# A hybrid decoder layer: the delta rule's outputs turned by VectorE instead of TensorE, one read back from memory, and a plan with other durations

## The chip, the cores and the metric

The kernel runs on one core of a Trainium2 chip. Its time is device microseconds from the start of the program to its end; the lower the better. Five engines work side by side, each on its own queue of instructions in order: TensorE (PE in the profile; it multiplies matrices, PEld is its weight load), VectorE (DVE), ScalarE (ACT), GpSimd (POOL) and SyncE (SP, which here only starts transfers). Transfers between the chip's memory (DRAM) and the on-chip memory (SBUF) run on 16 DMA engines. TensorE writes to PSUM, which VectorE and ScalarE read.

## What is computed

One decoder layer on 512 tokens of width 1024, in float32: a half-weighted SwiGLU block (width 2816), a mixer, a second SwiGLU block and a final norm. The mixer is one wide projection whose columns feed two branches:

- HGRN2: 8 heads of a gated linear recurrence, in chunks.
- Gated DeltaNet, the delta rule: 8 query/key heads and 16 value heads of 128, a causal short convolution on q, k and v, a decay for each head, and a chunked solve of a unit lower triangular system.

The part that the change touches is the second branch. In the reference, cut to what matters:

```python
T = triangular_solve(eye + A, eye, lower=True, unit_diagonal=True)
u = T @ (v * beta[..., None])
w = T @ (kb * exp(gam)[..., None])
def step(S, inp):                       # over the chunks of a head
    v_new = u_c - w_c @ S
    o = (q_c * exp(gam_c)[..., None]) @ S + qk_c @ v_new
    S = S * exp(g_end) + k_to_end.T @ v_new
...
o_g = rmsnorm(o_g, gdn_out_norm) * silu(gz)
y_g = o_g @ w_branch_gdn
y = sigmoid(gate_h) * y_h + sigmoid(gate_g) * y_g
```

## The kernel before, in words

Every float32 operand of a large product is split into a high and a low part of a rounded float32 type, and each product is three passes, high by high, low by high and high by low (`mm3`, L188 to L191). ScalarE makes the high part of a weight slab of 128 x 512 (`act.copy`, L1773) and VectorE the low part by a subtraction (L1783). For "folded" slabs ScalarE writes the negated high part instead (L1776), and a transfer started by POOL adds the slab from DRAM to it (L1779), so that VectorE has nothing to do. `folded` (L1789) decides: before, every second slab of the weights for k, q, v and z (48 slabs).

The layer has three stages: the first SwiGLU block (`ffn`), the mixer, the second block. The mixer is written as some 100 threads (Python generators) that ask for engines with a duration, for buffers and for events. `Desk` (L64 to L138) runs them against the durations that they state and so writes out, when the kernel is built, the order of the instructions on each engine; at run time the engines go through that order and wait for each other by semaphores. The durations are therefore what decides what stands where. `V` and `A` (L761, L762) give VectorE's and ScalarE's time from the number of elements, `T_` states TensorE's, and `LAG` (L52) the time that is left for transfers: `turn` for each leg of a detour through DRAM, `fold` for the adding transfer of a folded slab, `back`, `out`, `m` and others.

TensorE's dense products come from `product` (L1792) and `closing` (L1611), in a line that `loader` and `choose` set (weights through three raw buffers). Around them run the eight units of the delta rule (two value heads each):

- `g_n` (L1179) multiplies keys and queries (L1214) and masks the results on VectorE (L1218, L1220) and scales them (L1229).
- `g_b` (L1239) stores the four diagonal 32 x 32 blocks to DRAM, reads them back with a system in each partition (`gfs<-nb`, L1253) and the identity (L1259), and POOL solves them in 31 pairs of operations (L1265, L1266), whose time is stated as .78 + .0045 n w. The matrix has one buffer, `m`: unit u+1 is loaded when unit u has been solved (event `P`).
- `g_inv` (L1276) turns the solution on VectorE (L1284, L1291) and doubles it on TensorE twice, to blocks of 64 and 128 (L1308, L1318, L1331, L1339).
- `g_rec` (L1352) runs the recurrence over four chunks: L1393 and L1394 (state by keys and queries), L1397, L1406, L1411, L1420 and L1422, and the new state in L1433. Then the outputs are scaled by ScalarE (L1457), turned to the other layout by four TensorE transposes for each head (L1464), gated by VectorE (L1468) and stored (`keep`, `od<-on`); `operand` (L1545) reads them later for the branch's second product.
- The values come out of the convolution (`conv`, L1091) with channels in the partitions and are needed with tokens in them. VectorE turns blocks of 32 x 32 (`turn`, L1126), and `bounce` (L1128) stores the result (L1132) and reads it back in four transfers of a quarter each (L1138); `g_w` (L1269) multiplies it by its rate (L1273).

Of the kernel before, what the change touches and what calls it, by code (L numbers as in the profile page):

```python
# [8 lines left out]
F32 = mybir.dt.float32  # L9
F32R = mybir.dt.float32r  # L10
I32 = mybir.dt.int32
AF = mybir.ActivationFunctionType
ALU = mybir.AluOpType
# [4 lines left out]
T = 512  # L18
NT = T // P
D = 1024  # L20
# [28 lines left out]
STAY = (15,)  # L49
CONVS = 7  # L50
SLACK = 0.8
LAG = dict(raw=3.5, gb=6.5, nb=6, m=7, out=5, back=6, turn=2.5, fold=4.5)  # L52
EASE = 2.5
LANES = {"a": 2, "b": 2, "d": 1, "e": 1}

# [632 lines left out]
def mixer(tc, mp, e):  # L688
# [31 lines left out]
    for size, names in ((1024, "n2:2 gz:2 fs:1 ut:1"), (512, "kn:3 gm:1 qm:2 gb:2 ln:1 at:4 vb:4 t64:2 on:2"),  # L720
                        (256, "ft:1 tp:1 thg:2 x:1 we:1 s:3 w:1"), (128, "fm:1"), (64, "sm:4")):
        for it in names.split():
            n, b = it.split(":")
# [34 lines left out]

    D = Desk(wx0=1, wx1=1, wx2=1, wx3=1, mm=2, a=2, b=2, d=1, e=1, ta=TA, tm=6, thg=1, raw=RB, w=WB, n2=2, gz=2, fs=1, ut=1, t=3, kn=3, gm=1,
             qm=2, gb=2, ln=1, mi=3, mt=3, at=4, vb=4, t64=2, on=2, ft=1, x=1, we=1, w_=1, s=3)  # L760
    V = lambda n: ("use", "DVE", 0.21 + 0.001 * n)  # L761
    A = lambda n: ("use", "ACT", 0.2 + 0.0009 * n)  # L762
    T_ = lambda n: ("use", "PE", n)
    S = ("use", "SP", 0.4)

# [357 lines left out]

    def turn(out, x):

        dve.transpose(out.rearrange("p (f c j) -> p c f j", f=4, c=NT), x)  # L1126

    def bounce(name, x, out, tag=None):  # L1128

        yield S  # L1130
        scr = dr.tile([P, T], F32, name=name)
        sp.dma_start(scr, x)  # L1132
        yield "lag", LAG["turn"]
        if tag:
            D.put(tag)
        for f in range(4):
            yield S
            sp.dma_start(out[32 * f:32 * f + 32].rearrange("p (r a) -> p r a", r=4),  # L1138
                         scr.rearrange("(r i) (f a) -> f i r a", i=32, f=4)[f])
        yield "lag", LAG["turn"]  # L1140

    def g_e(u, st):
# [96 lines left out]
    def g_b(u, st):  # L1239


        n2 = st["n2"]
        nb = dr.tile([4, 8, 32, 32], F32, name=f"nb{u}")
        for b in range(4):
            r = slice(32 * b, 32 * b + 32)
            yield S
            sp.dma_start(nb[b].rearrange("s i j -> i s j"), n2[r, :, :, r].rearrange("p a c j -> p (a c) j"))
        yield "lag", LAG["nb"]
        yield "on", *([("P", u - 1)] if u else ["m"])
        m = G["m"][0]  # L1250
        for b in range(4):
            yield S
            sp.dma_start(m[32 * b:32 * b + 32].rearrange("p i j -> p (i j)"),  # L1253
                         nb[b].rearrange("s i j -> s (i j)").unsqueeze(0).to_broadcast([4, 8, 1024]))
        yield "on", ("t12", 0) if u % 3 else ("t0", 0)
        yield "get", "t", 1
        t = st["t"] = G["t12"][0][:, u % 3 - 1] if u % 3 else G["t0"][0]
        yield S
        sp.dma_start(t, eye4)  # L1259
        yield "lag", LAG["m"]  # L1260
        for j in range(31):
            n, w = 31 - j, j // 4 + 1
            yield "use", "POOL", .78 + .0045 * n * w
            tv = v3(places["fm"]("fm", (P, 96))[:, :n * w], n)
            pool.tensor_tensor(tv, bc(m[:, j + 1:, j], w), t[:, j:j + 1, :w].to_broadcast([P, n, w]), op=ALU.mult)  # L1265
            pool.tensor_tensor(t[:, j + 1:, :w], t[:, j + 1:, :w], tv, op=ALU.add)  # L1266
        D.fire(("P", u))
# [84 lines left out]
    def g_rec(u, st):  # L1352
# [99 lines left out]
        for i in range(2):  # L1452
            yield "get", "on", 1
            ons.append(places["on"]("on", (P, NT, P)))
            for c in range(NT):
                yield A(150)
                act.activation(ons[i][:, c], at[i][:, c], AF.Copy, scale=rho[:, 4 * i + c:4 * i + c + 1])  # L1457
        D.fire(("R", u))
        for i in range(2):
            yield "get", "b", 1  # L1460
            yield T_(Patient(.5))
            pt = ps("pto", "b")
            for c in range(NT):
                pe.transpose(pt[:, c * P:(c + 1) * P], ons[i][:, c], ident)  # L1464
            yield "on", ("z", 2 * u + i)
            yield V(560)
            og = ons[i].rearrange("p c b -> p (c b)")
            dve.scalar_tensor_tensor(og, pt, cs[:, C_GN:C_GN + 1], gz[:, i * T:i * T + T], op0=ALU.mult, op1=ALU.mult)  # L1468
            D.put("b")
            if i:  # L1470
                D.fire(("Z", u))
            if u == 7:
                yield "on", "projected"
                yield A(512)
                k = 14 + i
                a, b = so[k] = uh[:, k - 8], ul[:, k - 8]
                act.copy(a, og)
                yield V(512)
                dve.tensor_tensor(b, og, a.bitcast(F32), op=ALU.subtract)
                D.fire(("so", k))  # L1480
                continue
            D.start((6, u), keep(od[2 * u + i], og, "on", ("od", 2 * u + i)))

    def keep(to, tile_, tag, event=None):

# [22 lines left out]
    def zgate(i, pt):  # L1508

        yield "get", "ta", 1  # L1510
        yield *V(512), 1
        o = ta("zg")
        dve.tensor_tensor(o, pt, rbc, op=ALU.mult)
        D.put("mm")
        g = G["gz"][i // 2 % 3].rearrange("p c b -> p (c b)")[:, i % 2 * T:i % 2 * T + T]
        yield A(512)
        act.activation(g, o, AF.Tanh, scale=0.5)
        yield V(512)
        dve.scalar_tensor_tensor(g, g, 1.0, o, op0=ALU.add, op1=ALU.mult)
        D.put("ta")  # L1520
        D.fire(("z", i))
# [23 lines left out]
    def operand(k, wait, get, make):  # L1545

        yield "on", *wait
        if get:
            yield "get", get, 2
        yield "on", ("od", k), *([("so", k - 2)] if k > 10 else [])  # L1550
        yield "get", "ta", 1
        yield S
        og = ta("og")
        sp.dma_start(og, od[k])
        yield "lag", LAG["back"]
        if k > 8:
            yield "on", "projected"
        yield *A(512), 1
        a, b = so[k] = make()
        act.copy(a, og)  # L1560
        yield *V(512), 1
        dve.tensor_tensor(b, og, a.bitcast(F32), op=ALU.subtract)
        D.put("ta")
        D.fire(("so", k))

# [45 lines left out]
    def closing():  # L1611

        for d, q in wbgs:
            if q == 0:
                yield "get", "mm", 1
            yield "on", ("slab", (("m", d), q))
            hi, lo = made[("m", d), q]
            for j in range(4):
                k = 4 * q + j
                yield "on", ("so", k)  # L1620
                yield T_(.69)
                if k == 0:
                    pts[d] = psd.tile([P, T], F32, tag="mm", name="pmm")
                c = slice(j * P, (j + 1) * P)
                mm3(pts[d], hi[:, c], lo[:, c], *so[k], k == 0, k == VH - 1)
            D.put("w")
            if q == 3:
                D.fire(("wbg", d))
# [158 lines left out]
        D.fire(("slab", key))  # L1787

    def folded(k, q):  # L1789
        return k in 'kqvz' and q % 2  # L1790

    def product():  # L1792
        for n in range(len(todo) + len(gates) + len(line)):
            yield "on", ("line", n + 1)
            x = k, i = line[n]
            if k == "B":
                yield "get", "n2", 1
                hv_[i] = place("n2", "v", (P, NT, 256), 4)
                yield "get", "gz", 1
                hg_[i] = place("gz", "hg", (P, NT, 256), 4)  # L1800
                for t in range(NT):
                    yield "get", "mm", 1
                    for kt in range(KD):
                        if t == 0:
                            yield "on", ("slab", (x, kt))
                        yield T_(.69)
                        if kt == 0:
                            pt = psd.tile([P, T], F32, tag="mm", name="pnat")
                        ts = slice(t * P, (t + 1) * P)
                        mm3(pt, uh[:, kt, ts], ul[:, kt, ts], *made[x, kt], kt == 0, kt == KD - 1)  # L1810
                        if t == NT - 1:
                            D.put(f"wx{kt // 2}" if kt in EXTRA[i] else "w")
                    D.start((1, n), h_v(i, t, pt[:, :256]))
                    D.start((1, n), gate(("G", i), hg_[i], t, pt[:, 256:]))
                continue
# [15 lines left out]
            for q in range(2):  # L1831
                yield "on", ("slab", (x, q))
                hi, lo = made[x, q]
                for j in range(4):
                    kt = 4 * q + j
                    if k == "y":
                        yield "on", ("O", kt)
                    yield T_(.69)
                    if kt == 0:
                        pt = psd.tile([P, T], F32, tag="mm", name="pmm")  # L1840
                    a, b = o_h[kt] if k == "y" else ux(kt)
                    c = slice(j * P, (j + 1) * P)
                    mm3(pt, hi[:, c], lo[:, c], a, b, kt == 0, kt == KD - 1)
                D.put("w")
# [164 lines left out]
```

## Time and profile before

| | |
|---|---|
| time, median of 3 runs | 1617.11 us (1614.69 to 1617.34) |
| the profiled execution's own time | 1610.8 us |
| its span, first to last instruction | 1609.0 us |
| mean granted TensorE clock | 0.997 |
| packets and bytes of all transfers | 140258, 225.90 MB |

A row of the timeline has the start in us, the length in us, the engine, the line, the operation, what it writes and reads, the sizes, how many instructions were joined, and in brackets how long the engine stood idle before and what ended that. A row of the waits has who waited for whom, and the total, the number and the longest wait in us. A row for one line has the least, median and greatest duration in ns, and the first and last start. The chain of waits gives start, length and work of each piece that ended last.

### The profile page before, as it was taken

To read this page: it belongs to the slowest core of one execution; us is meant where nothing else is said; L and a number is where in the kernel's file an instruction comes from. 1 tells how busy PE (TensorE), PEld (TensorE's weight loads), DVE (VectorE), ACT (ScalarE), POOL (GpSimd) and SP (SyncE) were. 2 spreads that over 40 slices of the span, in tenths; PEclk is the share of its full clock that TensorE was granted. 3 is DMA by queue.
4 is the path that set the end of the run, shared out by engine and by line. 5 is a ranking of instruction groups with operands and counts; after the bars stand their busy time and mean duration, and the time that the engine had idled before them with its cause. 6 is when DMAs were issued, how large, how long until landed. Compare 5 with 4: busy or idle time off the path is not lost.

```text
span 1609.0 us, 29388 instructions
## 1 busy us (share of the span) xinstructions
PE 1590.0 (99%) x10608; PEld 1378.9 (86%) x10608; DVE 1128.4 (70%) x2227; ACT 859.7 (53%) x1920; POOL 453.7 (28%) x773
## 2 busy tenths in 40 slices
PE   9999999999999999999999999999999999999997
PEld 8999998888888888788878888788888899999887
DVE  6888785447787788657788888655545788878433
ACT  5766674332434446457777766555324666667222
POOL 0211212001121232257765667700001121121001
PEclk9999999999999999999999999999999999999999
DMA  5776863333422344576566666546544587786333
GB/s 183 170 162 155 180 162 102 120 109 86 106 54 61 90 109 108 161 175 159 142 181 158 149 160 183 153 151 190 160 142 131 137 182 159 156 186 147 92 90 117
DMA packets 140258, 225.90 MB, mean 140 GB/s; under 512 B 23232, under 2 KB 37312, under 8 KB 140112
## 3 DMA queue, kind: packets, MB, share of 16 engines
q1 hardware_dynamic: 116208, 180.80, 37.3%
q0 software_dynamic: 21312, 38.81, 15.8%
q10 hardware_dynamic: 2592, 4.42, 0.9%
q8 instruction: 83, 1.36, 0.4%
q14 instruction: 63, 0.52, 0.1%
HBM read 204.79 MB, written 19.17 MB: 139 GB/s over the span
## 4 chain that ended last, share of the span: by engine, by line
PE 84%; DMA 7%; issue 4%; DVE 3%; ACT 0%; SPq 0%; POOL 0%; POOLq 0%; DVEq 0%; ACTq 0%
PE pmm L189 18%; PE pmm L191 18%; PE pmm L190 18%; PE px L191 5%; PE px L190 5%; PE px L189 5%; DMA wlo<-w1a 2%; DMA wlo<-w1b 2%; PE pnat L189 2%; PE pnat L190 2%; PE pnat L191 2%; PE pgq L1214 1%; PE pog L1422 1%; PE pw L1406 1%; DMA gvb<-vn 1%
## 5 line engine op out<-in xcount | busy, mean ns | idle before, releaser
L189 PE MATMUL pmm<-uh,whi 128*128 128x512 f32 x879 | 361.6, 411 | 0.5 <-ACT whi L606 0.5
L191 PE MATMUL pmm<-uh,wlo 128*128 128x512 f32 x879 | 343.0, 390 | 0.0
L190 PE MATMUL pmm<-ul,whi 128*128 128x512 f32 x879 | 342.0, 389 | 0.0
L191 PE MATMUL px<-xs,wlo 128*128 128x256 f32 x1008 | 285.8, 284 | 0.9 <-DMA wlo<-w1b 0.8
L189 PE MATMUL px<-xs,whi 128*128 128x256 f32 x1008 | 285.2, 283 | 0.0
L190 PE MATMUL px<-xs,whi 128*128 128x256 f32 x1008 | 285.2, 283 | 0.0
L1773 ACT CAST whi<-raw 128x512 fp32r<-128x512 f32 x226 | 140.1, 621 | 214.0 <-PE pmm L190 164.1
L1783 DVE TENSOR_TENSOR wlo<-raw,whi 128x512 fp32r<-128x512 f32 x178 | 125.1, 703 | 102.5 <-ACT whi L1773 94.3
L191 PEld LDWEIGHTS pmm<-uh,wlo 128*128 128x128 f32 x879 | 165.0, 188 | 36.2
L191 PEld LDWEIGHTS px<-xs,wlo 128*128 128x128 f32 x1008 | 193.5, 192 | 1.9 <-DMA wlo<-w1b 1.1
L189 PEld LDWEIGHTS px<-xs,whi 128*128 128x128 f32 x1008 | 193.5, 192 | 0.1
L190 PEld LDWEIGHTS px<-xs,whi 128*128 128x128 f32 x1008 | 193.5, 192 | 0.1
L189 PEld LDWEIGHTS pmm<-uh,whi 128*128 128x128 f32 x879 | 165.4, 188 | 31.5 <-ACT whi L606 0.7
L190 PEld LDWEIGHTS pmm<-ul,whi 128*128 128x128 f32 x879 | 165.7, 188 | 29.5 <-DVE ul L216 0.3
L329 ACT CAST whi<-sw 128x512 fp32r<-128x512 f32 x144 | 87.6, 613 | 92.4 <-DVE sw L366 72.6
L308 DVE TENSOR_TENSOR wlo<-raw,whi 128x512 fp32r<-128x512 f32 x100 | 77.7, 787 | 77.3 <-ACT whi L329 76.9
L329 ACT CAST whi<-raw 128x512 fp32r<-128x512 f32 x104 | 61.4, 592 | 127.4 <-PE pmm L190 93.9
L227 POOL TENSOR_TENSOR acc<-acc,sqt 128x512 f32<-128x512 f32 x18 | 23.4, 1300 | 320.1 <-ACT sqt L225 320.1
L308 DVE TENSOR_TENSOR wlo<-sw,whi 128x512 fp32r<-128x512 f32 x144 | 98.0, 681 | 0.0
L329 ACT CAST whi<-rw 128x512 fp32r<-128x512 f32 (+1 forms) x130 | 79.6, 613 | 27.5 <-PE px L190 14.0
L334 POOL DMA_DIRECT2D wlo<-w1b x53 | 45.8, 864 | 168.8 <-ACT wlo L333 118.1
L189 PE MATMUL pmm<-xs,whi 128*128 128x512 f32 (+1 forms) x238 | 89.8, 377 | 0.0
(475 smaller groups left out, 3351.6 us busy)
## 6 DMA issues: line engine op xcount, KB each, us to landing
raw<-wt SPq DMA_DIRECT2D x160, 256.0 KB
rw<-w1b SPq DMA_DIRECT2D x80, 256.0 KB
rw<-w1a SPq DMA_DIRECT2D x74, 256.0 KB
wlo<-w1b POOLq DMA_DIRECT2D x53, 256.0 KB, 4.9
wlo<-wt POOLq DMA_DIRECT2D x48, 256.0 KB, 4.8
wlo<-w1a POOLq DMA_DIRECT2D x47, 256.0 KB, 5.1
raw<-w2b SPq DMA_DIRECT2D x41, 256.0 KB
raw<-w2a SPq DMA_DIRECT2D x36, 256.0 KB
```

The lines of the kernel that those rows point to most:

```text
L189: pe.matmul(pt, ah, bh, start=first, stop=False)
L190: pe.matmul(pt, ah, bl, start=False, stop=False)
L191: pe.matmul(pt, al, bh, start=False, stop=last)
L227: add.tensor_tensor(acc, acc, s, op=ALU.add)
L308: dve.tensor_tensor(lo, x, hi.bitcast(F32), op=ALU.subtract)
L329: act.copy(hi, x)
L334: pool.dma_start(lo, units[i].fold, accum_op=ALU.add)
L1214: pe.matmul(pq[:, (c % 2) * 256:(c % 2) * 256 + 256], kq[:, c, 0], kq[:, c].rearrange("p a b -> p (a b)"), start=True, stop=True)
L1406: pe.matmul(pw[:, hd2[i]], ut[:, 4 * i + c], xs[i], start=True, stop=True)
L1422: pe.matmul(po[:, 256 + i * P:256 + (i + 1) * P], at[i][:, c], w[:, hd2[i]], start=True, stop=True)
L1773: act.copy(hi, raw)
L1783: dve.tensor_tensor(lo, raw, hi.bitcast(F32), op=ALU.subtract)
```

## The change

In four parts:

- The outputs of 7 of 8 units (14 of 16 heads) no longer go through TensorE. ScalarE scales them in place, VectorE turns them in blocks of 32 x 32 (`turn`), and a new thread, `gated`, sends them through DRAM (`bounce`), gates them and keeps them. Unit 7 goes the old way.
- `turn` reads its input with a step of four elements, so that a block holds every fourth column, and writes blocks in order. Thereby `bounce` needs a single read, in which a partition gets four rows of 512 bytes. The kept outputs stand in another order of columns; `zgate` writes the gate in that order and `operand` reads it back in the plain one. The time for each leg in the plan goes from 2.5 to 5.
- The folded slabs are every second one of v, z, t, k and q: the 16 of the gates (t) are new, 64 in all, and the plan's time for their transfer goes from 4.5 to 5.
- The stated durations: VectorE 0.20 + .00096 n for 0.21 + .001 n, ScalarE 0.17 + .0009 n for 0.2 + .0009 n, a dense product .705 for .69, a pair of the POOL solve .6 + .0042 n w for .78 + .0045 n w. With them the whole order of the mixer is written anew.

```diff
-LAG = dict(raw=3.5, gb=6.5, nb=6, m=7, out=5, back=6, turn=2.5, fold=4.5)
+LAG = dict(raw=3.5, gb=6.5, nb=6, m=7, out=5, back=6, fold=5, turn=5)
...
-    V = lambda n: ("use", "DVE", 0.21 + 0.001 * n)
-    A = lambda n: ("use", "ACT", 0.2 + 0.0009 * n)
+    V = lambda n: ("use", "DVE", 0.20 + 0.00096 * n)
+    A = lambda n: ("use", "ACT", 0.17 + 0.0009 * n)
...
     def turn(out, x):
-        dve.transpose(out.rearrange("p (f c j) -> p c f j", f=4, c=NT), x)
+        dve.transpose(out.rearrange("p (f c j) -> p f c j", f=4, c=NT), x.rearrange("p (c i f) -> p f c i", c=NT, f=4))
...
-        for f in range(4):
-            yield S
-            sp.dma_start(out[32 * f:32 * f + 32].rearrange("p (r a) -> p r a", r=4),
-                         scr.rearrange("(r i) (f a) -> f i r a", i=32, f=4)[f])
+        yield S
+        sp.dma_start(out.rearrange("p (r a) -> p r a", r=4), scr.rearrange("(r i) (f a) -> (i f) r a", r=4, f=4))
         yield "lag", LAG["turn"]
...
-            yield "use", "POOL", .78 + .0045 * n * w
+            yield "use", "POOL", .6 + .0042 * n * w
...
             ons.append(places["on"]("on", (P, NT, P)))
+            to = at if u < 7 else ons
             for c in range(NT):
                 yield A(150)
-                act.activation(ons[i][:, c], at[i][:, c], AF.Copy, scale=rho[:, 4 * i + c:4 * i + c + 1])
+                act.activation(to[i][:, c], at[i][:, c], AF.Copy, scale=rho[:, 4 * i + c:4 * i + c + 1])
+            if u < 7:
+                yield V(512)
+                turn(ons[i].rearrange("p c b -> p (c b)"), at[i].rearrange("p c b -> p (c b)"))
         D.fire(("R", u))
         for i in range(2):
+            og = ons[i].rearrange("p c b -> p (c b)")
+            if u < 7:
+                D.start((6, u), gated(u, i, og, gz))
+                continue
...
+    def gated(u, i, og, gz):
+        yield from bounce(f"on{2 * u + i}", og, og)
+        yield "on", ("z", 2 * u + i)
+        yield V(560)
+        dve.scalar_tensor_tensor(og, og, cs[:, C_GN:C_GN + 1], gz[:, i * T:i * T + T], op0=ALU.mult, op1=ALU.mult)
+        D.fire(("z", u, i))
+        if ("z", u, 1 - i) in D.at:
+            D.fire(("Z", u))
+        yield from keep(od[2 * u + i], og, "on", ("od", 2 * u + i))
...
-        dve.tensor_tensor(o, pt, rbc, op=ALU.mult)
+        x, y, z = (v.rearrange("p (c r j) -> p c r j", r=4, c=NT) for v in (o, pt, rbc))
+        if i < 14:
+            x = o.rearrange("p (r c j) -> p c r j", r=4, c=NT)
+        dve.tensor_tensor(x, y, z, op=ALU.mult)
...
-        act.copy(a, og)
+        g4, a4, b4 = og.rearrange("p (r c j) -> p r c j", r=4, c=NT), *(x.rearrange("p (c r j) -> p r c j", r=4, c=NT) for x in (a, b))
+        act.copy(a4, g4)
         yield *V(512), 1
-        dve.tensor_tensor(b, og, a.bitcast(F32), op=ALU.subtract)
+        dve.tensor_tensor(b4, g4, a4.bitcast(F32), op=ALU.subtract)
...
-                yield T_(.69)
+                yield T_(.705)
...
     def folded(k, q):
-        return k in 'kqvz' and q % 2
+        return k in 'vztkq' and q % 2
```

More of the change, by code (lines that the diff above doesn't have):

```diff
@@ L1466, in g_rec @@
             yield V(560)
-            og = ons[i].rearrange("p c b -> p (c b)")
             dve.scalar_tensor_tensor(og, pt, cs[:, C_GN:C_GN + 1], gz[:, i * T:i * T + T], op0=ALU.mult, op1=ALU.mult)
@@ L1805, in product @@
                             yield "on", ("slab", (x, kt))
-                        yield T_(.69)
+                        yield T_(.705)
                         if kt == 0:
@@ L1837, in product @@
                         yield "on", ("O", kt)
-                    yield T_(.69)
+                    yield T_(.705)
                     if kt == 0:
```

## The prediction

> **What bounds the kernel now.** I read the page's busy shares first, then the waits of TensorE, then the stage of the eight delta-rule units by itself.
>
> ```profile
> PE 1590.0 (99%) x10608; PEld 1378.9 (86%) x10608; DVE 1128.4 (70%) x2227; ACT 859.7 (53%) x1920; POOL 453.7 (28%) x773
> ...
> POOL 0211212001121232257765667700001121121001
> ```
> ```profile
> 719.60:1057.30 337.70, 334.23 (x2197) 274.85 (x2198) 269.12 (x599) 233.53 (x663) 225.32 (x480) 1.00 0.62 161
> ```
>
> TensorE is the bound; the kernel can only gain by taking work from TensorE or by ending its waits. The second row is the stretch from the first unit's inverse to the last's (columns: length, then busy PE, weight loads, DVE, ACT, POOL, clock, DMA share, GB/s). DVE is busy for 269 of 338 us there, so what it is made to wait for matters.
>
> ```profile
> PE pgq L1214 <- DVE gqm L1220: 3.5, 2, 3.2
> PE pks L1393 <- DVE s L1433: 2.1, 1, 2.1
> ```
> ```profile
> DVE gvb L1273 <- DMA gvb<-vn: 26.2, 10, 5.5
> ```
> ```profile
> 679.05 0.69 DVE L1273 TENSOR_TENSOR gvb<-gvb,sm 128x512 f32<-128x512 f32 x1 [2.71 <-DMA gvb<-vn]
> 679.66 0.42 DVE L1220 TENSOR_TENSOR gqm<-pgq,sq 128x256 f32<-128x256 f32 x1
> ```
> ```profile
> 1011.56 0.69 DVE L1273 TENSOR_TENSOR gvb<-gvb,sm 128x512 f32<-128x512 f32 x1 [4.94 <-DMA gvb<-vn]
> 1012.17 0.60 DVE L1433 SCALAR_TENSOR_TENSOR s<-s,gx,pog 128x128 f32<-128x128 f32 x2
> ```
>
> The two longest waits of TensorE in the mixer, 3.2 and 2.1 us, name L1220 and L1433. Both are the next instruction on DVE behind L1273, which stood there for a value that had not come back through memory. So the real releaser is the values' transfer: DVE lost 26.2 us to it in ten waits, and TensorE 5.3.
>
> A second loop runs beside TensorE: the 32x32 solves on POOL. Unit u+1 cannot start before unit u is done and its matrix is loaded (one buffer, `m`).
>
> ```profile
> 712.86 0.20 POOL L1266 TENSOR_TENSOR gft<-gft,fm 128x8 f32<-128x8 f32 x1
> ```
> ```profile
> 715.13 0.71 DVE L1284 STREAM_TRANSPOSE gtp<-gft 128x256 f32<-128x256 f32 x1
> ```
> ```profile
> 719.64 0.69 PE L1308 MATMUL pq<-gut,gn 32*32 32x32 f32 x32
> ```
> ```profile
> 852.11 0.20 POOL L1266 TENSOR_TENSOR gft<-gft,fm 128x8 f32<-128x8 f32 x1
> ```
> ```profile
> 871.44 0.55 POOL L1265 TENSOR_TENSOR fm<-gfs,gln 128x31 f32<-128x31 f32 x1
> 872.07 0.28 POOL L1266 TENSOR_TENSOR gln<-gln,fm 128x31 f32<-128x31 f32 x1
> 872.43 0.57 POOL L1265 TENSOR_TENSOR fm<-gfs,gln 128x30 f32<-128x30 f32 x1
> ```
> ```profile
> 999.51 0.59 POOL L1266 TENSOR_TENSOR gft<-gft,fm 128x8 f32<-128x8 f32 x1
> ...
> 1010.32 0.25 POOL L1265 TENSOR_TENSOR fm<-gfs,gln 128x31 f32<-128x31 f32 x1 [2.51 <-DMA gvb<-vn]
> ...
> 1013.89 0.79 POOL L1265 TENSOR_TENSOR fm<-gfs,gln 128x54 f32<-128x54 f32 x1
> ...
> 1018.71 0.88 POOL L1779 DMA_DIRECT2D wlo<-wt  x1 [0.25 <-ACT wlo L1776]
> 1019.32 0.61 POOL L1265 TENSOR_TENSOR fm<-gfs,gln 128x69 f32<-128x69 f32 x1
> ...
> 1028.12 1.67 POOL L1449 TENSOR_TENSOR sm<-sm,mhalf 128x8 f32<-128x8 f32 x1
> 1029.78 0.57 POOL L1265 TENSOR_TENSOR fm<-gfs,gln 128x75 f32<-128x75 f32 x1
> ```
> ```profile
> 1043.62 0.20 POOL L1266 TENSOR_TENSOR gln<-gln,fm 128x8 f32<-128x8 f32 x1
> ```
> ```profile
> 1057.26 0.69 PE L1308 MATMUL pq<-h,gn 32*32 32x32 f32 x32
> ```
>
> The first solve ends at 713.1, the eighth at 1043.8: 330.8 us for seven periods. One pause was long (852.3 to 871.4, 19.1 us); the usual one is that from 1000.1 to 1010.3, 10.2 us. Without the 8.9 us of excess, **POOL's period is 46.0 us**. The last solve alone is 33.5 us (1010.3 to 1043.8) with one transfer and one power inside. TensorE takes L1308 at 719.6 and, seven units on, at 1057.3: 337.6 us, 48.2 a unit. So POOL is ready 6.6 us before the first inverse and 13.4 before the last; no wait of TensorE on a solve exists. That margin is what the change spends.
>
> **The change, part by part** (against the profiled execution, 1610.8 us; span 1609.0).
>
> *Outputs off TensorE.* 14 of 16 heads lose four transposes each (L1464).
>
> ```profile
> 1070.60 0.66 PE L1464 MATMUL pto<-sq,on 128*128 128x128 f32 x4
> 1071.01 0.48 PE L189 MATMUL pmm<-uh,whi 128*128 128x512 f32 x1
> 1071.33 0.39 PE L190 MATMUL pmm<-ul,whi 128*128 128x512 f32 x1
> 1071.56 0.39 PE L191 MATMUL pmm<-uh,wlo 128*128 128x512 f32 x1
> ```
>
> From start to start a group takes 0.41 us, and the product behind it starts its second pass 0.32 later instead of 0.23: 0.50 us. 14 x 0.50 = **-7.0 us**. In their place stand 14 DVE turns, 14 stores and 14 reads. These outputs are read by the branch's second product: in the changed order more than 80 us of TensorE work lies between unit 6's last output and the first product that reads it, so the detour costs nothing; without that cover it would cost its two transfers and the keeping. The gating waits on DVE for the read; behind it there stand the next unit's slab subtractions and state updates, for which TensorE waits. The chain of waits shows a store of 3.4 us and a slow read of 5.5:
>
> ```profile
> 672.05 3.40 DMA vn<-ci
> ...
> 1005.95 5.49 DMA gvb<-vn
> ```
>
> The plan's two legs of 5 us hold the sum, 8.9, so I add no wait. The traffic grows by 14 x 0.5 MB and 16 x 0.25 MB, some 11 MB on engines that are busy for 0.62 of the stretch.
>
> *Values: one read, more time.* The four quarter reads become one, and the plan puts 5 us in place of 2.5 on each leg. The 26.2 us of waits should go, and TensorE's 5.3 with them: **-5.3 us** (bounds: 0 if the one read lands late, 6.6 if shorter waits go too). SP issues 64 - 16 = 48 reads fewer, and 28 transfers more for the outputs. What is late next? The solve.
>
> *Sixteen more folded slabs.* Each moves one DVE subtraction to an ACT multiply and a POOL transfer. Twelve come after the last solve, where POOL is idle (the last row of the page's extract, in slices of 40 us, is 0 or 1 from slice 27 on), four before. I cost this at nothing: the slabs have time until they are used; were that gone, each could cost its landing, which I leave to the range.
>
> *Durations.* The solve is charged .6 + .0042 nw instead of .78 + .0045 nw per pair; with nw summing to 1560 over 31 pairs that is 25.2 us instead of 31.2. The trace does not bear this out: from 871.44 to 872.43 one pair takes 0.99 us where the new formula says 0.73, and unit 7's 33.5, less 0.6 for its transfer (1018.71 to 1019.32) and 1.7 for its power (1028.12 to 1029.78), is 31.2. **The old figure was right**, and the plan now sets TensorE's inverses by solves 6 us too short. Its order shows this: products (0.69 us each, three starts 0.23 apart) between one L1308 and the next are 49, 52, 47, 60, 46, 47, 47 before (348) and 42, 39, 60, 48, 45, 44, 43 after (321). Of the 337.6 us before, 348 x 0.69 = 240.1, twelve transpose groups are 6.0 and the wait of L1393 is 2.1; the other 89.4 are 12.8 a unit. So TensorE's periods after are 41.8, 39.7, 54.2, 45.9, 43.9, 43.2, 42.5, and against POOL's 46.0 it comes early by 4.2, 6.3, -8.2, 0.1, 2.1, 2.8, 3.5.
>
> ```profile
> L1126 DVE STREAM_TRANSPOSE ci<-cy x16: 693/711/712, 657.9 to 1024.5; 128x512 f32<-128x512 f32 x16
> ```
> ```profile
> L1291 DVE STREAM_TRANSPOSE gut<-gtp x8: 422/435/441, 715.9 to 1004.9; 32x256 f32<-32x256 f32 x8
> ```
>
> From a solve's end to its inverse the least is 2.1 (713.1 to L1284) + 0.7 + 4 x 0.435 = 4.6 us, so the first unit has 6.6 - 4.6 = 2.0 spare. The walk: 2.2 of wait at unit 1, 6.3 at unit 2; unit 3 gains 8.2, of which I let half be kept (its scores are multiplied behind unit 1's inverse, so its solve can't start much earlier); units 4 and 5 use 2.2 of the 4.1, unit 6 waits 0.9, unit 7 3.5. Sum **+12.9 us** (bounds: 8.8 with all spare time used, 19.0 with none).
>
> *Sharing with POOL.* A POOL step takes 0.25 where DVE stands still (1010.32) and 0.79 beside the tap sums L1105 (1013.89), which read two SBUF tensors. Gating an output now reads two as well, where it read PSUM and one. Twelve such operations in the stretch, 0 to 0.54 each: I take half, **+3.2** (bounds 0 and 6.5). The Trainium skill (SBUF - State Buffer, Who interferes with whom) says that a Vector instruction with two SBUF inputs contends with a GpSimd instruction that reads SBUF; these rows agree.
>
> *Turns.* 12 turns of 0.71 are added to DVE in the stretch (8.5 us in 338, 80% to 82%), and every turn now reads with a step of four elements. No row shows such a read by itself: 0.71 if free (L1126). L1284, strided on both sides, takes 0.71 for half the elements where L1291 takes 0.435 for as many, so at worst 512 elements cost 0.71 + 2 x 0.275 = 1.26. DVE has room for either; 0 in the sum.
>
> Sum: -7.0 - 5.3 + 12.9 + 3.2 = +3.8, 1614.6 for a run like the profiled one. The median of the runs shown, 1617.1, lies 6.3 above it; so **1621 us**.
>
> **The rivals.**
>
> *The solves don't gate: faster.* While DVE waits for a solve, POOL's steps fall towards 0.25, and if a solve comes near the plan's 25.2, POOL's period is 46.0 - 6.0 = 40.0 and only unit 2 is late, by 0.3. Then -12.3: 1605. For it: the 0.25 row. Against: DVE stops only for the last few us of each solve.
>
> *The two cancel: within 0.2%.* All spare time is used (8.8) and gating costs POOL little: -3.5 to 0, 1614 to 1617.
>
> *DVE becomes the bound: slower.* If a turn takes 1.26, the 26 turns of the stretch add 14.3 us, and DVE needs 269 + 8.5 + 14.3 = 292 of some 324 us, 90%, beside its waits for the solves. It decides once these waits pass the 32 us left; then the 14 us come on top: 1635. Against: DVE's own 26 us of waits go. The Trainium skill (SBUF - State Buffer, Door 1) says that SBUF is read in lines of 16 bytes and that each access in a new line pays; a step of four fp32 is a new line each time. By it the rival's 1.26 would hold; L1284 agrees but can't tell reading from writing.
>
> *The change doesn't do what it says.* The single read of 512 short rows lands later than 5 us and L1273 still waits: 5.3 come back, 1626.
>
> **How the numbers follow.** Forecast (the solves gate, by about the sum) 0.38; cancel 0.17; faster 0.28; DVE 0.10; late read 0.07. A measurement of this kernel can tell about 0.2%, 3.2 us. Slower 0.38 + 0.10 + 0.07 = 0.55, within 0.17, faster 0.28. The range goes from the faster rival to DVE's, 1605 to 1636.
>
> **What would show it.** The waits of TensorE should name L1308's solve or what stands behind L1284 on DVE, at units 1, 2 and 7; DVE's list should have L1282 of the new file (the old L1284) behind POOL in place of L1273 behind DMA; POOL's period should stay near 46 and a pair near 1.0. Transposes of outputs fall from 64 to 8. The turn's duration decides between 0.71 and 1.26. If TensorE's inverse never waits, or solves fall below 30 us, the forecast is wrong on the fast side; if TensorE waits on DVE where no solve is due, DVE is the bound.

## The result, and the profile after

The changed kernel takes 1643.49 us (median of 5 runs, 1642.70 to 1646.68): slower than before by a ratio of 1.0162 (95% interval 1.0139 to 1.0185). The forecast was 1621 with a range to 1636: the sign was right, the size was not. The profiled execution took 1643.49 us too, its span was 1641.6 (before 1609.0), and its mean granted clock 0.987 (before 0.997).

In the changed file the quoted lines of the old one between L1139 and L1450 stand two earlier: L1282 turns the solution (old L1284), L1306 and L1316 are the inverse (L1308, L1318), L1263 and L1264 the pairs of the solve (L1265, L1266), L1251 loads the matrix (L1253), L1271 scales the values (L1273). New are L1126 for the outputs as well, L1494 (the gating) and L1503 (the store of a kept output, od<-on). In `solve_short` and `short_on3_kept`, two of the experiments below, two added lines shift the solve and all behind it back to the old numbers.

First the page of the changed kernel, busy shares and POOL by slices, then the stretch from the first inverse to the last, in the columns of the row shown of before.

```profile
PE 1596.3 (97%) x10552; PEld 1381.0 (84%) x10552; DVE 1135.1 (69%) x2225; ACT 868.7 (53%) x1936; POOL 454.6 (28%) x789
...
POOL 0211222002122132466475566611001121121001
```
```profile
713.50:1066.90 353.40, 322.55 (x2060) 261.99 (x2060) 273.96 (x593) 229.97 (x649) 220.25 (x486) 0.95 0.65 169
```

The 56 output transposes are gone (10608 - 56 = 10552 instructions on PE). Yet the stretch is 353.4 us long where it was 337.7; TensorE has 137 instructions fewer in it, stands idle for 30.9 us (before 3.5), and runs at a mean clock of 0.95 (before 1.00). Over the whole span TensorE is idle for 45.3 us instead of 19.0: 26.3 of the 32.6 us. The clock was halved in six stretches between 754 and 1065 us, 34.1 us together. For 9.9 us of them TensorE stood idle, where a halved clock costs nothing, as in the row below (columns as above; busy PE 0.00, clock 0.50):

```profile
974.00:978.00 4.00, 0.00 (x0) 0.00 (x0) 1.04 (x5) 1.79 (x7) 1.85 (x6) 0.50 0.19 73
```

In the other 24.2 us it worked at half speed, which costs 12.1 us; before, there was one such stretch of 3.4 us, which cost at most 1.7. (Both kernels also end with some 7 us at half clock.) So 26.3 of idle time and 10.4 of clock, less transposes, at most 7.0, make 29.7 of the 32.6 us. The spans differ by more than the medians (26.4) because the profiled execution before was 6.3 us faster than the median of its kernel.

The waits of TensorE in the changed kernel, 600 to 1120 us, the longest four:

```profile
PE pq L1316 <- ACT acc L1309: 8.3, 2, 8.1
PE pog L1418 <- DVE x L1409: 7.1, 2, 6.4
PE pog L1418 <- DVE gwe L1409: 6.1, 2, 4.0
PE pw L1404 <- DVE x L1271: 4.1, 1, 4.1
```

No row names a solve. The waits of VectorE and of SP's queue do:

```profile
DVE gvb L1271 <- DMA gvb<-vn: 12.0, 3, 7.3
DVE x L1282 <- POOL gln L1264: 10.8, 3, 5.5
DVE on L1126 <- DMA od<-on: 8.9, 3, 4.2
```
```profile
SPq L1251 <- POOL gln L1264: 17.1, 2, 10.5
...
SPq L1503 <- DVE on L1494: 10.7, 5, 7.7
```

VectorE (L1282) and SP (L1251) both stand for the solve, and both go through their instructions in order. What TensorE waits for is what stands behind them. Three places in the timelines show the paths; whether a late solve is needed for each is a matter for the experiments.

**Directly.** VectorE stands 5.5 us for the second solve, and the correction of the state behind it (L1409) comes 4.0 us late for TensorE:

```profile
751.55 0.66 DVE L1282 STREAM_TRANSPOSE x<-gln 128x256 f32<-128x256 f32 x1 [5.51 <-POOL gln L1264]
```
```profile
753.90 1.10 PE L1418 MATMUL pog<-gwe,gkn 128*128 128x256 f32 x2 [4.01 <-DVE gwe L1409]
```

**Through the buffers of the outputs, and back to POOL.** There are two `on` buffers, held from the turn until the kept output has been stored. SP issues the stores at 816.8; VectorE stands at the next turn until 823.7. Behind this turn stands L1190, which POOL needs for a power (L1193), and behind that power stands the next solve:

```profile
816.76 0.85 SPq L1503 DMA_DIRECT2D od<-on  x2
```
```profile
823.66 1.10 DVE L1126 STREAM_TRANSPOSE on<-gat 128x512 f32<-128x512 f32 x1 [4.24 <-DMA od<-on]
824.68 0.13 DVE L1190 TENSOR_SCALAR sm<-sm 128x4 f32<-128x4 f32 x1
```
```profile
794.33 0.21 POOL L1264 TENSOR_TENSOR gln<-gln,fm 128x8 f32<-128x8 f32 x1
...
824.89 1.46 POOL L1193 TENSOR_TENSOR sm<-sm,mhalf 128x4 f32<-128x4 f32 x1 [1.65 <-DMA x<-vn]
826.35 0.24 POOL L1263 TENSOR_TENSOR fm<-gfs,gft 128x31 f32<-128x31 f32 x1
```

The bracket of L1193 names a read that came last by the profile; the row that it can't do without is L1190, which ends at 824.8. Between two solves POOL pauses for 31.8 us here (794.5 to 826.35). So a late output pushes the next solve back. That a late solve made this output late is not shown: with short solves (`solve_short` below) VectorE stands at the same turn for as long, and the pause is as long.

**Through SP.** The matrix of the next unit can be loaded only when the sixth solve has ended (963.6). Behind this load stands the read og<-od, behind that read ScalarE, and behind ScalarE the inverse. The read is slow as well: SP issues it at 967.2, and ScalarE goes on at 976.2.

```profile
963.35 2.62 SPq L1251 DMA_DIRECT2D gfs<-nb  x4
...
967.16 0.43 SPq L1573 DMA_DIRECT2D og<-od  x1
```
```profile
976.20 0.62 ACT L1580 CAST sogb<-og 128x512 fp32r<-128x512 f32 x1 [6.80 <-DMA og<-od]
...
977.32 0.72 ACT L1309 COPY acc<-pq 32x256 f32<-32x256 f32 x2
```
```profile
968.27 0.39 PE L191 MATMUL pmm<-uh,wlo 128*128 128x512 f32 x1
968.50 0.39 PE L189 MATMUL pmm<-uh,whi 128*128 128x512 f32 x1
...
978.09 1.06 PE L1316 MATMUL pq<-acc,x 32*32 32x32 f32 x32 [8.06 <-ACT acc L1309]
...
981.28 0.63 PE L189 MATMUL pmm<-uh,whi 128*128 128x512 f32 x1
981.70 0.63 PE L190 MATMUL pmm<-ul,whi 128*128 128x512 f32 x1
```

The last rows also show the price after a wait: before it passes start 0.23 us apart, after it 0.42.

### The profile page after: what moved, and what is told of

Its sections match the earlier page's. It is cut to its first block, busy times and chain, and to the rows that moved or that the text cites. A ratio compares the mean times of both kernels' runs of the same rounds, so it can differ in the third digit from the quotient of the medians.

```text
span 1641.6 us, 29286 instructions
## 1 busy us (share of the span) xinstructions
PE 1596.3 (97%) x10552; PEld 1381.0 (84%) x10552; DVE 1135.1 (69%) x2225; ACT 868.7 (53%) x1936; POOL 454.6 (28%) x789
## 5 line engine op out<-in xcount | busy, mean ns | idle before, releaser
L189 PE MATMUL pmm<-uh,whi 128*128 128x512 f32 x879 | 365.4, 416 | 0.4 <-ACT uh L1580 0.4
L191 PEld LDWEIGHTS pmm<-uh,wlo 128*128 128x128 f32 x879 | 166.6, 190 | 36.5
L190 PEld LDWEIGHTS pmm<-ul,whi 128*128 128x128 f32 x879 | 167.5, 191 | 30.9 <-DVE ul L1582 0.6
L1803 DVE TENSOR_TENSOR wlo<-raw,whi 128x512 fp32r<-128x512 f32 x162 | 113.7, 702 | 113.7 <-ACT whi L1793 107.1
L308 DVE TENSOR_TENSOR wlo<-raw,whi 128x512 fp32r<-128x512 f32 x100 | 77.7, 788 | 76.5 <-ACT whi L329 76.1
L1799 POOL DMA_DIRECT2D wlo<-wt x64 | 56.4, 881 | 162.6 <-ACT wlo L1796 66.6
```

What stands on the lines that cost most here:

```text
L189: pe.matmul(pt, ah, bh, start=first, stop=False)
L190: pe.matmul(pt, ah, bl, start=False, stop=False)
L191: pe.matmul(pt, al, bh, start=False, stop=last)
L308: dve.tensor_tensor(lo, x, hi.bitcast(F32), op=ALU.subtract)
L1799: pool.dma_start(lo, src, accum_op=ALU.add)
L1803: dve.tensor_tensor(lo, raw, hi.bitcast(F32), op=ALU.subtract)
```

## The experiments

All ratios are against the kernel before, measured on the same chip; its medians in the batches were 1612 to 1617 us, so ratios are compared, not microseconds across batches. Span and clock are those of the one profiled execution; in solve_short, short_on3_kept, on3_kept and durations_alone it was the fastest of its kernel's runs, so their spans come out a little low. "Order kept" means that each engine's instructions stand as in the changed kernel (less those left out).

| kernel | median us | ratio (95%) | span | clock |
|---|---|---|---|---|
| changed | 1643.49 | 1.0162 (1.0139 to 1.0185) | 1641.6 | 0.987 |
| solve_old | 1608.13 | 0.9972 (0.9960 to 0.9983) | 1604.8 | 0.998 |
| durations_alone | 1658.06 | 1.0283 (1.0257 to 1.0310) | 1653.5 | 0.989 |
| outputs_on_pe | 1631.14 | 1.0111 (1.0087 to 1.0134) | 1629.8 | 0.991 |
| on3 | 1631.33 | 1.0117 (1.0094 to 1.0140) | 1632.5 | 0.991 |
| solve_short, order kept | 1618.50 | 1.0032 (1.0014 to 1.0050) | 1612.5 | 0.994 |
| old_pe | 1611.54 | 0.9992 (0.9978 to 1.0005) | 1609.9 | 0.997 |
| old_turn_on3 | 1620.29 | 1.0045 (1.0030 to 1.0060) | 1619.5 | 0.992 |
| solve_more | 1618.00 | 1.0035 (1.0023 to 1.0047) | 1617.0 | 0.993 |
| on3_kept, order kept | 1635.68 | 1.0130 (1.0096 to 1.0163) | 1632.3 | 0.992 |
| short_on3_kept, order kept | 1613.47 | 1.0000 (0.9981 to 1.0018) | 1608.7 | 0.996 |
| values_alone | 1612.44 | 0.9982 (0.9967 to 0.9997) | 1612.2 | 0.996 |
| solve_mid | 1618.84 | 1.0017 (0.9999 to 1.0035) | 1617.6 | 0.997 |

The theory: the short charge for the solve sets the order wrong, and lateness is passed on. The rivals: the outputs' detour, or VectorE's time, is the loss by itself.

**solve_old**: the changed kernel with the old charge.

```diff
-            yield "use", "POOL", .6 + .0042 * n * w
+            yield "use", "POOL", .78 + .0045 * n * w
```

> The changed kernel with the solve on POOL charged as before, .78 + .0045 nw, all else as changed. If the solve that is charged 6 us too little is the cause, the inverses stand far enough apart again and the time comes back to 1605 to 1620 us, with no wait of VectorE on the solve. If the outputs' buffers (two, held from the turn to the landing of the kept output) are the cause, 1630 to 1645 remain.

Measured 0.9972: one constant takes back 1.9%, and the rest of the change is worth 0.3%. VectorE waits for no solve, as expected. Its waits of TensorE in the same window, the first and longest; and the stretch between its first and last inverse:

```profile
PE pog L1418 <- ACT wlo L1796: 1.1, 1, 1.1
```
```profile
719.80:1048.00 328.20, 323.36 (x2114) 263.35 (x2113) 275.63 (x594) 232.72 (x659) 230.49 (x487) 1.00 0.70 189
```

TensorE does 54 instructions more between its inverses than in the changed kernel, in 25 us less. VectorE is as busy as there (276 us), so VectorE's work isn't the bound.

**durations_alone**: the kernel before with the four stated durations of the change, outputs and values as before.

```diff
-    V = lambda n: ("use", "DVE", 0.21 + 0.001 * n)
+    V = lambda n: ("use", "DVE", 0.20 + 0.00096 * n)
...
-            yield "use", "POOL", .78 + .0045 * n * w
+            yield "use", "POOL", .6 + .0042 * n * w
```

> The kernel before with the four stated durations alone changed. If the short solve is the cause: slower than before by 10 to 25 us. If the outputs' buffers are: within 5 us of before, 1612 to 1622.

Measured 1.0283, more than the whole change, and 46 us above the kernel before in its batch where the theory had 10 to 25: the way is as the theory has it, the size is not, and why it is larger than in the changed kernel stays open. The same waits stand there with no detour and no slower turn; VectorE for the solve, TensorE for what is behind it:

```profile
DVE gtp L1284 <- POOL gln L1266: 7.2, 1, 7.2
DVE x L1284 <- POOL gln L1266: 6.1, 2, 5.7
```
```profile
PE pks L1393 <- DVE s L1433: 8.4, 2, 6.8
PE pog L1420 <- DVE gwe L1411: 7.1, 3, 5.9
```

**outputs_on_pe**: the changed kernel with all outputs turned by TensorE, as before.

```diff
-            if u < 7:
-                D.start((6, u), gated(u, i, og, gz))
-                continue
```

> The changed kernel with the outputs turned by TensorE as before; values, slabs and durations as changed. If the short solve is the cause, it stays at 1630 to 1650 us (7 us of transposes come back). If the outputs' detour through memory with its two buffers is the cause, it comes to 1610 to 1620.

Measured 1.0111, within the span that the theory gave: without any detour of the outputs a loss of 1.1% stays, and VectorE still stands 6.9 us in two waits for a solve (L1282). Beside the changed kernel it is 0.5% faster, but each has an order of its own, and such a difference is weakly founded (see old_turn_on3 below). **old_pe** is the same beside the old charge:

> The changed kernel with the solve charged as before and the outputs turned by TensorE as before. Beside the run with the old charge and the turned outputs, 1608.1, it tells what the turned outputs are worth: 7 us of transposes if they come whole, so 1615; 1608 or less if the turns on VectorE and the detour cost as much as they save.

Measured 0.9992 against 0.9972 for solve_old: beside the right charge the detour seems to gain 0.2%, too little to tell across two orders.

**on3** gives the outputs a third buffer and lets the plan know.

```diff
-             qm=2, gb=2, ln=1, mi=3, mt=3, at=4, vb=4, t64=2, on=2, ft=1, x=1, we=1, w_=1, s=3)
+             qm=2, gb=2, ln=1, mi=3, mt=3, at=4, vb=4, t64=2, on=3, ft=1, x=1, we=1, w_=1, s=3)
```

> The changed kernel with three buffers for the outputs instead of two. If the buffers are the cause, the waits of VectorE's turn on the kept output's store go and the time falls to 1615 to 1628 us. If the short solve is the cause, 1635 to 1645 remain.

Measured 1.0117; 1631.3 us lies between the two expected spans. But the plan wrote another order, so this run can't tell the buffer from the order. **on3_kept** can: the memory has three buffers, the plan counts two.

```diff
-    for size, names in (... (512, "kn:3 gm:1 qm:2 gb:2 ln:1 at:4 vb:4 t64:2 on:2"),
+    for size, names in (... (512, "kn:3 gm:1 qm:2 gb:2 ln:1 at:4 vb:4 t64:2 on:3"),
```

> The changed kernel with a third buffer for the outputs that come back through memory, and the order of the instructions on every engine as it is (the plan still counts two). If the two buffers pass the lateness on, VectorE's wait of 8.9 us for a kept output to land goes, and with it TensorE's of 4.3 and part of that of 6.6: 1632 to 1638 us. Rival: the 12 us that three buffers gave with a new order came from the new order; VectorE then stands at the next thing that is late, and the time stays at 1640 to 1645.

Measured 1635.68, within the expected span of the theory. By the ratios (1.0130 for 1.0162) that is 0.3%, some 5 us, and the two intervals overlap; the medians differ by 7.8 us, the spans by 9.3. The waits are clearer: VectorE's for a kept store falls from 8.9 to 1.7 us, and TensorE's longest behind it (L1409) from 6.4 to 2.6, while VectorE still waits for the solve:

```profile
DVE on L1126 <- DMA od<-on: 1.7, 2, 1.4
DVE x L1282 <- POOL gln L1264: 7.7, 3, 4.8
```
```profile
PE pog L1418 <- DVE x L1409: 3.3, 2, 2.6
```

**solve_short**: the order as it is, and the solves really shorter: the last 6 of 31 pairs are left out, so the solutions are incomplete.

```diff
+            if j > 24:
+                continue
```

> The changed kernel with its order of instructions untouched, but the last six of the 31 pairs of each solve left out (the solve is then incomplete), so that a solve really takes about the 25 us that the plan states. If the lateness of the solve itself causes the time: 1598 to 1612 us and no wait of VectorE on a solve. If the new order is bad for another reason: 1630 or more.

Measured 1.0032: with the same instructions in the same order on the other engines, 1.3 of the 1.62% are gone, some 21 of 26 us. No wait of VectorE on a solve is left, as expected; the time, 1618.5, is 6.5 above the theory's span. Two waits of 4 us are left, and VectorE's wait for the kept stores:

```profile
PE pog L1420 <- DVE x L1411: 4.0, 1, 4.0
PE pw L1406 <- DVE x L1273: 3.9, 1, 3.9
```
```profile
DVE on L1126 <- DMA od<-on: 6.6, 2, 4.1
```

At the place shown for the changed kernel, the third solve now ends at 780.6 and the fourth starts at 816.5, after a pause of 35.9 us, with the same wait at the turn. The row of L1193 names L1190 here:

```profile
780.35 0.28 POOL L1266 TENSOR_TENSOR gln<-gln,fm 128x49 f32<-128x49 f32 x1
...
815.05 1.46 POOL L1193 TENSOR_TENSOR sm<-sm,mhalf 128x4 f32<-128x4 f32 x1 [1.51 <-DVE sm L1190]
816.50 0.25 POOL L1265 TENSOR_TENSOR fm<-gfs,gft 128x31 f32<-128x31 f32 x1
```
```profile
813.80 1.11 DVE L1126 STREAM_TRANSPOSE on<-gat 128x512 f32<-128x512 f32 x1 [4.08 <-DMA od<-on]
```

So this pause and the wait for a buffer belong to the order with two buffers, and need no late solve.

**short_on3_kept** has both, the shorter solves and the third buffer, in the same order; here too 6 of 31 pairs are left out.

> The changed kernel in its own order, with a third such buffer and the last 6 of 31 pairs of every solve left out, so that the solutions aren't complete. If late solves and the two buffers together are what the change lost, no wait of TensorE over 2 us is left in the stage and the time is that of the changed kernel with the old solve charge, 1606 to 1612 us. Rival: the order itself, with its uneven shares of products between the inverses, keeps a loss of its own: 1615 to 1619, as with the short solves alone.

Measured 1.0000; the median, 1613.5, lies 1.5 above the top of the theory's range, in a batch whose kernel before was 2 to 3 us slower than in the others. One wait of TensorE over 2 us is left, so this half of the expectation missed. It stands at the place shown under "Through SP", where it was 8.1: about half of that wait is the read's own, and not the solve's:

```profile
PE pq L1318 <- ACT acc L1311: 4.2, 1, 4.2
```
```profile
712.80:1033.20 320.40, 311.25 (x2059) 254.96 (x2058) 274.36 (x592) 229.50 (x646) 194.81 (x402) 0.99 0.71 186
```

The stretch does the work of the changed kernel's 353.4 us (2060 instructions) in 320.4. By the ratios the buffer alone gives 0.3%, the short solves alone 1.3%, both 1.6%: together the whole loss. Beside solve_old 0.3% is left.

**solve_mid** and **solve_more** move the charge alone, halfway and above the old one.

```diff
-            yield "use", "POOL", .6 + .0042 * n * w
+            yield "use", "POOL", .69 + .00435 * n * w
```

> The changed kernel with a pair of the solve charged halfway, .69 + .00435 n w, 28.2 us a solve. If every microsecond that the charge is short costs alike, half of the 35 us between 1643 and 1608: 1623 to 1629. If the spare time before the inverse (6.6 us before the first one) covers a shortfall of 3 us and only what goes beyond it is paid: 1607 to 1613. If any lateness sets off the chain of buffers and halved clock: over 1633.

Measured 1.0017, 1618.8 us, between the bands and 0.45% slower than solve_old, where the full shortfall of 6 us costs 1.9%. VectorE waits for a solve only once, for 0.6 us, so the spare time covers a shortfall of 3 us here. What the 0.45% is stays open; VectorE stands 5.7 us for a kept store.

```diff
-            yield "use", "POOL", .6 + .0042 * n * w
+            yield "use", "POOL", .9 + .0045 * n * w
```

> The changed kernel with the solve charged .9 + .0045 nw, 34.9 us instead of 25.2. If only a charge below the traced 31 us hurts: within 4 us of 1608. If the time goes on falling with the charge, the solve's transfers and powers are charged too little as well: under 1604.

Measured 1.0035, 0.6% slower than solve_old. **old_turn_on3** (old charge, a turn charged 1.1 as traced, three buffers known to the plan) is 0.7% slower than it too. Both missed both of their expected spans.

```diff
-            yield V(512)
-            turn(th, y)
+            yield "use", "DVE", 1.1
+            turn(th, y)
```

> The changed kernel with the solve charged as before, the strided turn charged at its traced 1.1 us and three buffers for the outputs. If what is left of waits comes from the turn's length and the buffers: 1600 to 1606 us; if not, within 3 us of 1608.

Each has a wait to show: in solve_more TensorE stands 4.7 us for an inverse's first product (L1316 for L1309); in old_turn_on3 VectorE stands 5.8 us at the gating (L1494) for a read of the detour, which the plan has due in 5.

A statement nearer to the trace doesn't make a better order by itself. Two kernels whose orders the plan wrote anew differed by 0.6 to 0.7% here without a late solve, so effects below that, across orders, are weakly founded here; what rests on kept orders is not touched by it.

**values_alone**: the kernel before with the new `turn` and `bounce` for the values only, legs of 5.

```diff
-LAG = dict(raw=3.5, gb=6.5, nb=6, m=7, out=5, back=6, turn=2.5, fold=4.5)
+LAG = dict(raw=3.5, gb=6.5, nb=6, m=7, out=5, back=6, turn=5, fold=4.5)
```

> The kernel before with the new turn, the single read of the values and 5 us for each leg in the plan; outputs, folded slabs and other durations as before. The prediction's term was -5.3: 1606 to 1608 us, and VectorE's wait for the values falls from 26 us to under 10. Rival: the slower turn (16 times 0.4 us) and the new order take it back: 1610 to 1615 with the wait gone all the same. A second rival, that the single read lands late: the wait stays at 20 us or more.

Measured 0.9982, a gain of 0.2%, at the edge of what can be told; the time, 1612.4, and the fallen wait are what the rival expected. VectorE's wait for the values fell as expected (26.2 before):

```profile
DVE gvb L1271 <- DMA gvb<-vn: 7.4, 6, 2.7
```

The best kernel of all is solve_old: the change with the old charge, 0.3% faster than before.

## Why the prediction was right and wrong

**The solve's charge (+12.9, bounds 8.8 to 19.0): the right cause, mis-sized.** It cost 1.9%, some 31 us of the 1612 in that batch. The step that failed is the walk: it counts only waits straight behind a solve, and it holds "POOL's period is 46.0 us" fixed, as if TensorE could come early and POOL would go on at its pace.

Straight behind a solve the walk found two of its places: TensorE stood 4.0 us at unit 1 and 2.1 at unit 7 (forecast 2.2 and 3.5), but at unit 2, where 6.3 were forecast, not at all. The longer waits, 4.1, 6.4 and 8.1 us, stand behind the turn that needs a free buffer and behind SP's queue. The walk has neither. The prediction expected VectorE behind POOL at L1282, and it stands there (10.8 us); it did not ask what is queued behind L1251 on SP, nor what the detour's buffers hold up.

Nor did POOL keep its pace. From the first solve's end (706.4) to the eighth's (1057.1) there are 350.7 us, 50.1 a unit instead of 47.3 before and 46.0 in the forecast. The solves themselves didn't get longer, which the least, median and greatest durations show, before and after:

```profile
L1265 POOL TENSOR_TENSOR fm<-gfs,gln x155: 202/312/1094, 723.1 to 1043.0; 128x60 f32<-128x60 f32 x15, 128x28 f32<-128x28 f32 x10, 128x54 f32<-128x54 f32 x10, 128x48 f32<-128x48 f32 x10
```
```profile
L1263 POOL TENSOR_TENSOR fm<-gfs,gln x155: 203/302/1292, 718.6 to 1056.6; 128x60 f32<-128x60 f32 x15, 128x28 f32<-128x28 f32 x10, 128x54 f32<-128x54 f32 x10, 128x48 f32<-128x48 f32 x10
```

The pauses did: 31.8 us behind the third solve, where the prediction took 10.2 as the usual one and left the one long pause of before (19.1) out as an excess. They are not lateness; in solve_short that pause is 35.9. With 5.3 us less for each of its last seven solves, POOL's period there is 46.8, 3.3 less than in the changed kernel: a solve starts when the other engines have its input ready, so a shorter solve is followed by a longer pause, and POOL can't run ahead as the walk lets it at unit 3. The order with the right charge (solve_old) has no wait of VectorE on a solve at all.

**The clock, not priced at all.** After each wait of 4 us or more quoted of the changed kernel TensorE ran at half speed, and after shorter ones too. The first two rows are the wait of 4.0 us that ends at 753.9, the last two one of 1.7 us that ends at 1029.6:

```profile
749.00:754.00 5.00, 0.99 (x5) 0.52 (x5) 2.35 (x6) 0.21 (x1) 2.87 (x7) 1.00 0.45 60
754.00:757.00 3.00, 3.00 (x9) 2.13 (x9) 2.83 (x7) 2.02 (x7) 0.00 (x0) 0.50 0.82 166
```
```profile
1027.00:1030.00 3.00, 1.28 (x18) 0.81 (x18) 2.20 (x6) 2.93 (x9) 2.53 (x7) 1.00 0.69 109
1030.50:1033.50 3.00, 3.00 (x8) 2.31 (x7) 2.81 (x7) 1.91 (x4) 2.77 (x5) 0.50 0.56 179
```

The 26.3 us of added idle time brought some 10 us of slower work with them (the sum above), so a wait of TensorE is to be counted at more than its length. The Trainium skill (TensorE: Matmul & The Clock Gate, What's actually happening) says that the clock has two states, and that an idle window of about 3.4 us drops it to half until the array has been busy for another. The two states and the length agree: the six stretches last 3.4, 6.8 or 10.2 us. The idle time that it takes does not: here 1.7 and 2.1 us were followed by half clock, while 2.6 us in on3_kept and 2.1 in the kernel before were not.

**Outputs off TensorE (-7.0): not told apart.** old_pe against solve_old gives 0.2%, some 3 us, in the forecast's sense, but less than two orders can differ by. "The detour costs nothing" failed in the changed kernel: the prediction looked for a reader that might wait (more than 80 us away, and none did), and not for the buffer that the detour holds. on3_kept gives 0.3% for it, and VectorE's wait of 8.9 us shows it.

**Values (-5.3): the waits went (26.2 to 7.4 in values_alone), the gain is about half**, 0.2%, 2.9 us. In the changed kernel 12.0 us of that wait are back. The late solves don't explain it, since solve_old has 12.9; why they are back stays open.

**Sharing with POOL (+3.2): the mechanism shows, its price on the time was not tested.** Before, a step of POOL beside a gating that reads PSUM took 0.31 us; after, one beside a gating that reads two tensors in SBUF took 0.82:

```profile
785.90 0.31 POOL L1265 TENSOR_TENSOR fm<-gfs,gln 128x72 f32<-128x72 f32 x1
```
```profile
785.88 0.73 DVE L1468 SCALAR_TENSOR_TENSOR on<-pto,cs,ggz 128x512 f32<-128x512 f32 x1
```
```profile
955.93 0.82 POOL L1264 TENSOR_TENSOR gln<-gln,fm 128x48 f32<-128x48 f32 x1
```
```profile
955.87 0.74 DVE L1494 SCALAR_TENSOR_TENSOR on<-on,cs,ggz 128x512 f32<-128x512 f32 x1
```

Of the solve's steps that start during a gating, those before took 0.22 to 0.33 us, those after 0.57 to 0.82 but for one of 0.25. Eight steps at some 0.3 us more each, an estimate from these rows, are 2 to 3 us on POOL over the eight solves; the medians of all steps above can't show so few.

**Turns (0 in the sum): right.** The turn with a step of four takes 1.10 us instead of 0.71, between the two bounds:

```profile
L1126 DVE STREAM_TRANSPOSE ci<-cy x16: 1084/1102/1136, 637.0 to 1041.0; 128x512 f32<-128x512 f32 x16
```

The rival "VectorE is the bound" is out: solve_old has the same turns and gains. The rule of the Trainium skill behind that rival (SBUF - State Buffer, Door 1), a new line of 16 bytes for each element, points the right way; the price is 0.39 us for 512 elements, not the 0.55 of the rival.

**Sixteen more slabs (0):** not tried alone. In solve_old the longest wait of TensorE in the stage, 1.1 us, names a folded slab's row (L1796); more than that does not show. (The prediction calls the row of POOL 0 or 1 from slice 27 on; it has two slices of 2 there.)

**The faster rival** needed solves near 25 us and had POOL's period fall to 40.0 with them. In the changed kernel they took 29.6 to 36.5 us. Made shorter (solve_short, 23.9 to 31.3 us), they left the period at 46.8 and the time at 1.0032, and with the third buffer at 1.0000: the period doesn't fall with the solve.

**What stays open.** Why solve_mid, solve_more and old_turn_on3 each lose 0.5 to 0.7% beside solve_old was read from their waits and not tested; nor was it tested how the 1.3% for late solves divides between the waits straight behind them, SP's queue and the clock.

## What to carry to other kernels

Where a plan with stated durations sets the order, a charge that is too short costs more than the waits straight behind the late result: list, for each engine or queue that will stand for it, what is queued behind it. Don't hold the pace of an engine fixed when its input comes from the others. A detour through memory is to be checked for the buffer that it holds as well as for its reader. And a wait of TensorE can cost its length and a halved clock behind it; here waits from 1.7 us on did, though not all. Compare ratios rather than the spans of single profiled executions.

## What the runs showed of the hardware

- After waits of TensorE of 1.7, 2.1, 4.0, 4.1, 6.4 and 8.1 us in the changed kernel the granted clock was 0.50 in stretches of 3.4, 6.8 or 10.2 us, some of which began within the wait; passes of 128x512 started 0.42 to 0.43 us apart in them instead of 0.23. Waits of 2.6 us (on3_kept) and 2.1 us (before) were not followed by it.
- A 32x32-block transpose of 128x512 fp32 on VectorE takes 1.10 us when it reads with a step of four elements and writes in order, 0.71 when it reads in order and writes strided blocks.
- A step of the solve on POOL that started while VectorE gated an output from two tensors in SBUF took 0.57 to 0.82 us (one of nine 0.25); while VectorE gated from PSUM and one tensor in SBUF, 0.22 to 0.33 us.
